# A hybrid decoder step on one core: the first three projection blocks computed together, a quarter of the contraction at a time

## The chip, the cores and the metric

The kernel runs on one core of one Trainium2 chip. The metric is the time of one execution on the device in microseconds (us); of several runs the median is taken. A profile is a separate, recorded execution; its span goes from the first to the last instruction of the core.

The engines by the names that the profile uses: PE is the matrix engine, PEld its weight loads, DVE the vector engine, ACT the scalar engine, POOL the general engine, SP the engine whose queue issues the transfers (SPq).

## The reference, cut to what matters

One layer of a decoder for 304 tokens (16 meta, 256 prompt, 32 sample tokens) of width 2048. The part that the change touches is the very beginning: a norm over the features, and the first columns of the input projection.

```
def rmsnorm(x, g):
    y = x * lax.rsqrt(jnp.mean(x * x, axis=-1, keepdims=True) + EPS)
    return y * g
...
proj = rmsnorm(x, g_mix) @ w_in          # 2048 -> 9248 columns
gate_lru, x_lru, z, xbc_raw, dt_raw = ...   # 2048, 2048, 2048, 3072, 32 columns
xbc = silu(causal_conv(xbc_raw, ...))    # x, B, C of the SSD part
dt = jax.nn.softplus(dt_raw + dt_bias)   # 32 heads
```

After it come the SSD scan, a gated linear recurrence (RG-LRU), an output projection, a squared-ReLU MLP with 8192 hidden features and a final norm. Everything is float32 to float32 accuracy.

## The kernel before, in words

Features lie on the 128 partitions, tokens in the columns. A projection is cut into **blocks** of 128 output features. A block is a sum over 16 feature tiles `k` of 128; since the matrix engine is fed with rounded values (type fp32r), weights and activations are each split into a high part and a low rest, and each `k` takes three matmuls of 128x304: high x high, high x low, low x high. A block is thus 48 matmuls into one bank of the accumulator memory (`gemm`, the matmul is L101).

`prep` brings the weights of a block: a transfer into one of two buffers `wraw` (L78), then ACT makes `whi` (helper `act`, L69) and DVE makes `wlo = wraw - whi` (helper `tt`, L58). `whi` and `wlo` have four buffers of 8 tiles `k`, two for each block. `run_blocks` asks for the weights two blocks ahead. A transfer into `wraw` must wait until ACT and DVE have read the block that lay there.

At the start the input `x` comes in 16 transfers (tiles `big`, L205), one per `k`. The first blocks take x as it comes: ACT makes `x0h` = x times the norm's gain, rounded; DVE makes `x0l`, the rest, in one instruction (helper `stt`, L61). The 1/rms of each token, `rsb`, is multiplied onto the results later. For it the squares of x are summed into `sqx`: eight squares and three additions on POOL, then eight squares on ACT that DVE adds. Matmuls with a column of ones (L161) and a broadcast (L172) turn the sum into `rsb`; only then can the results that are held back be worked on (the posts: `post_dt`, `post_conv`), and the normalized operands `xh`, `xl` of all later blocks be made, in what time DVE has left.

The first block is dt, 32 columns wide. Before, these are copied four times side by side, so that dt is a block like any other, 48 matmuls. Then come the blocks B (`win[0]` to `win[3]`), C and the first four of x. The step size chain on dt (`tables`: softplus, scan, transposes) follows when the held results are released.

The order on each engine is set by a scheduler that orders instructions by a timeline of its own; what it made of both programs is shown with the change. The names with numbers in those rows are single tiles; the profile leaves the numbers out.

Of the kernel before, what the change touches and what calls it, by code (L numbers as in the profile page):

```python
# [28 lines left out]
# columns of the constants  # L29
# [4 lines left out]
def body(ctx, tc, I, O):  # L34
# [38 lines left out]
    # ---------------------------------------------------------------- weights  # L73
# [33 lines left out]
    # blocks: (weights, operands, first column, last column, what follows)  # L107
# [35 lines left out]
    # ---------------------------------------------------------------- constants  # L143
# [14 lines left out]
    # ---------------------------------------------------------------- RMS norm  # L158
# [26 lines left out]
    sqa = sqx[:, 0, :]  # L185
    held, scaled = [], []
# [8 lines left out]
    parts = []  # L195
    for k in range(NK):
        if k % 8 == 0:
            parts.append([wp.tile([P, 8, P], F32R, tag=t, bufs=4, name=nm(t)) for t in ("whi", "wlo")])
        if k % 4 == 0:
            r = rdt[:, k:k + 4, None, :].to_broadcast([P, 4, 4, 32])  # L200
            wh, wl = [t[:, k % 8:k % 8 + 4, :].rearrange("p k (c j) -> p k c j", j=32) for t in parts[-1]]
            act(wh, r, AF.Copy)
            tt(V if k < 8 else G, wl, r, wh.bitcast(F32), SUB)
        xt = bigt()
        SY.dma_start(xt[:], I["x"][:, k, :])  # L205
        xts.append(xt)
        gm = par[:, C_GMIX + k:C_GMIX + k + 1]
        hi = x0p.tile([P, T], F32R, tag="xh", name=nm("x0h"))
        lo = x0p.tile([P, T], F32R, tag="xl", name=nm("x0l"))
        act(hi[:], xt[:], AF.Copy, scale=gm)  # L210
        stt(lo[:], xt[:], gm, hi[:].bitcast(F32), MUL, SUB)
        x0.append((hi, lo))
        if k < 8:
            tt(G, sqx[:, k, :], xt[:], xt[:], MUL)
    for n in (4, 2, 1):
        tt(G, sqx[:, 0:n, :], sqx[:, 0:n, :], sqx[:, n:2 * n, :], ADD)
    ready[id(wdt)] = parts

    def norm_x():
        for k in range(8, NK):  # L220
            sq = sp.tile([P, EXT], F32, tag="th", bufs=2, name=nm("sq"))
            act(sq[:, :T], xts[k][:], AF.Square)
            tt(V, sqa, sqa, sq[:, :T], ADD)
        for _ in range(7):
            yield
# [26 lines left out]
    # ---------------------------------------------------------------- other resident data  # L252
# [9 lines left out]
    hw = cst.tile([P, 152], F32, name="hw")      # halves of conv_ssd_w, conv_ssd_b; lru_ba, lru_bx  # L262
# [42 lines left out]
    # ---------------------------------------------------------------- SSD: B, C, x  # L305
    bf = [sp.tile([P, T], F32, tag="bf", bufs=4, name=f"bf{g}") for g in range(4)]
    cf = [sp.tile([P, T], F32, tag="cf", bufs=4, name=f"cf{g}") for g in range(4)]
# [759 lines left out]
```

## Time and profile before

| | |
|---|---|
| time of 3 runs, median | 1652.5 us (1652.13 to 1656.11) |
| span of the profiled execution | 1649.8 us |
| PE busy | 1625.4 us, 99% of the span |
| DVE, ACT, POOL busy | 64%, 50%, 15% |
| mean granted clock of PE | 0.995 of full speed |
| moved from and to memory | 260.0 and 12.4 MB, 165 GB/s over the span |

The profiled execution's own time is 2.7 us shorter in its span than the median of the runs; what lies around the span is not shown. PE is busy nearly always, so a change can gain or lose only where PE waits or runs at a lower clock: that is at the start (the page cuts the span into 40 slices; PE's digit is 7 in the first and 9 in nearly all others), in one wait of 3.0 us at 126 us, and in the last slice.

### The profile page before, as it was taken

The page shows a single profiled execution, that of the slowest core. Times are in us where ns is not written, and L with a number is a line of the kernel's source. Part 1 is how long each engine was busy: PE and PEld are TensorE (multiplying, and loading weights), DVE is VectorE, ACT ScalarE, POOL GpSimd, SP SyncE. Part 2 cuts the span into 40 slices and gives each one's busy share as a digit, 9 for nine tenths or more (in the row PEclk, how much of TensorE's full clock was granted, in tenths as well). Part 3 has the DMA queues.
Part 4 walks back from the last instruction along what each step waited for, and adds up shares of the span by engine and source line. Part 5 has one row for each costly group of instructions (what it writes and reads, how often), then busy time and mean ns, then how long its engine had stood idle before and what let it go on. Part 6 is the DMA issues. An engine that isn't in the chain of part 4 may idle for free.

```text
span 1649.8 us, 29019 instructions
## 1 busy us (share of the span) xinstructions
PE 1625.4 (99%) x11915; PEld 1587.4 (96%) x11915; DVE 1048.4 (64%) x1542; ACT 830.7 (50%) x1299; POOL 248.0 (15%) x311
## 2 busy tenths in 40 slices
PE   7999999999999999999999999999999999999997
PEld 6998888889999999999999999999999999999997
DVE  7989898988778787556565433544445555545554
ACT  5546575566777775344444433443334433344442
POOL 3433443431223221001140000000000000000000
PEclk9999999999999999999999999999999999999998
DMA  6444555554444455544545444454545454544442
GB/s 215 156 167 139 187 180 180 175 186 142 164 161 164 163 169 180 190 168 160 172 154 170 162 162 170 160 172 157 176 156 176 155 169 163 169 164 161 171 157 105
DMA packets 53989, 274.29 MB, mean 166 GB/s; under 512 B 5984, under 2 KB 12768, under 8 KB 24544
## 3 DMA queue, kind: packets, MB, share of 16 engines
q1 hardware_dynamic: 53856, 272.44, 48.9%
q8 instruction: 93, 1.52, 0.4%
q14 instruction: 40, 0.33, 0.1%
HBM read 259.99 MB, written 12.42 MB: 165 GB/s over the span
## 4 chain that ended last, share of the span: by engine, by line
PE 98%; DMA 1%; DVE 0%; SPq 0%; ACT 0%; issue 0%; DVEq 0%; ACTq 0%
PE g L101 90%; PE s L101 1%; PE s L439 1%; PE s L764 1%; PE s L562 1%; PE s L560 1%; PE s L501 1%; PE s L437 0%; PE s L510 0%; DMA wraw<-in_win 0%; PE s L161 0%; PE s L449 0%; DVE z L58 0%; PE s L172 0%; PE s L521 0%; PE s L587 0%
## 5 line engine op out<-in xcount | busy, mean ns | idle before, releaser
L58 DVE TENSOR_TENSOR wlo<-wraw,whi 128x1024 fp32r<-128x1024 f32 (+1 forms) x470 | 573.3, 1221 | 443.8 <-ACT whi L69 443.2
L69 ACT ACTIVATE whi<-wraw 128x1024 fp32r<-128x1024 f32 (+1 forms) x470 | 492.4, 1049 | 683.6 <-PE g L101 630.3
L101 PE MATMUL g<-mh,whi 128*128 128x288 f32 x1024 | 303.2, 296 | 0.0
L101 PE MATMUL g<-hh,whi 128*128 128x288 f32 x1024 | 303.0, 296 | 0.0
L101 PE MATMUL g<-hl,whi 128*128 128x288 f32 x1024 | 302.4, 295 | 0.0
L101 PE MATMUL g<-ml,whi 128*128 128x288 f32 x1024 | 302.1, 295 | 0.0
L101 PE MATMUL g<-hh,wlo 128*128 128x288 f32 x1024 | 301.3, 294 | 0.0
L101 PE MATMUL g<-mh,wlo 128*128 128x288 f32 x1024 | 301.1, 294 | 0.0
L101 PE MATMUL g<-xh,whi 128*128 128x288 f32 (+1 forms) x960 | 288.3, 301 | 3.0 <-DVE ext L288 3.0
L101 PE MATMUL g<-xl,whi 128*128 128x288 f32 (+1 forms) x960 | 287.4, 300 | 0.0
L101 PE MATMUL g<-xh,wlo 128*128 128x288 f32 (+1 forms) x960 | 286.8, 299 | 0.0
L101 PEld LDWEIGHTS g<-mh,wlo 128*128 128x128 f32 x1024 | 192.9, 188 | 0.0
L101 PEld LDWEIGHTS g<-hh,wlo 128*128 128x128 f32 x1024 | 192.8, 188 | 0.0
L101 PEld LDWEIGHTS g<-hh,whi 128*128 128x128 f32 x1024 | 192.5, 188 | 0.0
L101 PEld LDWEIGHTS g<-hl,whi 128*128 128x128 f32 x1024 | 192.5, 188 | 0.0
L101 PEld LDWEIGHTS g<-ml,whi 128*128 128x128 f32 x1024 | 192.3, 188 | 0.0
L101 PEld LDWEIGHTS g<-mh,whi 128*128 128x128 f32 x1024 | 191.9, 187 | 0.0
L101 PEld LDWEIGHTS g<-xh,whi 128*128 128x128 f32 x960 | 180.3, 188 | 6.9 <-DVE ext L288 3.2
L101 PEld LDWEIGHTS g<-xl,whi 128*128 128x128 f32 x960 | 180.4, 188 | 3.9 <-issue 1.0
L101 PEld LDWEIGHTS g<-xh,wlo 128*128 128x128 f32 x960 | 180.6, 188 | 2.8 <-issue 0.2
L101 PE MATMUL g<-lh,whi 128*128 128x288 f32 x256 | 75.8, 296 | 0.0
L101 PE MATMUL g<-sh,whi 128*128 128x288 f32 x256 | 75.7, 296 | 0.0
(272 smaller groups left out, 2327.7 us busy)
## 6 DMA issues: line engine op xcount, KB each, us to landing
wraw<-in_win SPq DMA_DIRECT2D x69, 1024.0 KB, 5.0
wraw<-in_wup SPq DMA_DIRECT2D x64, 1024.0 KB, 4.9
wraw<-in_wdn SPq DMA_DIRECT2D x64, 1024.0 KB, 4.9
wraw<-in_wout SPq DMA_DIRECT2D x32, 1024.0 KB, 4.9
h<-in_stssd SPq DMA_DIRECT2D x32, 256.0 KB, 3.0
out_sssd<-h SPq DMA_DIRECT2D x32, 256.0 KB, 3.5
wraw<-in_win SPq DMA_DIRECT2D x12, 256.0 KB, 5.2
big<-in_x SPq DMA_DIRECT2D x16, 152.0 KB, 3.6
```

The source lines that it names most:

```text
L58: e.tensor_tensor(out, a, b, op=op)
L69: A.activation(out, in_, f, **kw)
L101: TE.matmul(o, a[:, k % 8, :], b[:, c0:c1], start=n == 0, stop=n == 3 * NK - 1)
L439: TE.matmul(po[0:66, :], cm[:, 66 * b:66 * b + 66], a[:], start=b == 0 and n == 0, stop=b == 7 and n == 1)
L501: TE.matmul(pbc[:, 0:NT], selr[:, h:h + 1].to_broadcast([64, P]), acst[:], start=True, stop=True)
L560: TE.matmul(py[64 * q:64 * q + 64, 128 * c:128 * c + 128], xdc[c][:, 64 * j:64 * j + 64], em[c][:, j, :], start=True, stop=True)
L562: TE.matmul(py[:, 256 + 128 * c:384 + 128 * c], hst[c][:, 128 * t:128 * t + 128], C[:, 16 + 128 * c:144 + 128 * c], start=True, stop=True)
L764: TE.matmul(pr[:, :FL], w_[:, m, :], x_[:], start=n == 0, stop=n == 2)
```

## The change

It alters the start only; later parts are the same code (comments were dropped, so line numbers move).

- dt's high and low parts lie side by side: one operand `wd` of 64 columns for each `k` (66 are taken, the last two belong to the next tile). Each `k` takes two matmuls, with `x0h` and `x0l`, instead of three; dt is 32 matmuls. Its result has two halves of 32 rows, which `tables` adds and copies four times in one float32 matmul with a selection matrix (`s4`, `px`).
- dt, `win[0]` and `win[1]` run together (`run_first`): a quarter of the contraction (4 `k`) of dt, then of `win[0]`, then of `win[1]`, then the next quarter. Loads follow that order: 4 tiles of x, a quarter of the weights of both blocks, and so on; so do the splits on ACT and DVE.
- `x0l` is made in two DVE instructions: `xg` = x times gain (one operand tile, one buffer), then `xg - x0h`.
- The squares of the last eight tiles are made by ACT into the still unused tiles `bf`, `cf`, early, and all eight are added by POOL, not DVE. POOL's two instructions for dt's `wlo` go.
- Nine float32 matmuls of 128x128 on ones run at the very start (`wps`), before any data is there.
- `norm_x` takes fewer steps before the sum of squares is used, `tables` one more.

```diff
+    wps = bank()
+    for _ in range(9):
+        TE.matmul(wps[:, 0:P], ones[:].to_broadcast([P, P]), ones[:].to_broadcast([P, P]), start=True, stop=True)
...
+    first = [[], []]
+    wd = x0p.tile([P, 64 * NK + 2], F32R, tag="wd", bufs=1, name="wd")
+    wd3 = wd[:, 0:64 * NK].rearrange("p (k j) -> p k j", j=64)
...
     for k in range(NK):
-        if k % 8 == 0:
-            parts.append([wp.tile([P, 8, P], F32R, tag=t, bufs=4, name=nm(t)) for t in ("whi", "wlo")])
-        if k % 4 == 0:
-            r = rdt[:, k:k + 4, None, :].to_broadcast([P, 4, 4, 32])
-            wh, wl = [t[:, k % 8:k % 8 + 4, :].rearrange("p k (c j) -> p k c j", j=32) for t in parts[-1]]
-            act(wh, r, AF.Copy)
-            tt(V if k < 8 else G, wl, r, wh.bitcast(F32), SUB)
...
+        if m == 0:
+            wh, wl = wd3[:, k:k + 8, 0:32], wd3[:, k:k + 8, 32:64]
+            act(wh, rdt[:, k:k + 8, :], AF.Copy)
+            tt(V, wl, rdt[:, k:k + 8, :], wh.bitcast(F32), SUB)
...
         act(hi[:], xt[:], AF.Copy, scale=gm)
-        stt(lo[:], xt[:], gm, hi[:].bitcast(F32), MUL, SUB)
+        V.tensor_scalar(xg[:], xt[:], gm, None, op0=MUL)
+        tt(V, lo[:], xg[:], hi[:].bitcast(F32), SUB)
         x0.append((hi, lo))
         if k < 8:
             tt(G, sqx[:, k, :], xt[:], xt[:], MUL)
+        else:
+            act((bf + cf)[k - 8][:], xt[:], AF.Square)
+        if k % 4 == 3:
+            q = slice(k - 3, k + 1)
+            for f, raw, ap in zip(first, raws, win):
+                SY.dma_start(raw[:, q, :], ap[:, q, :])
+                wh, wl = [t[:, m - 3:m + 1, :] for t in f[-1]]
+                act(wh, raw[:, q, :], AF.Copy)
+                tt(V, wl, raw[:, q, :], wh.bitcast(F32), SUB)
     for n in (4, 2, 1):
         tt(G, sqx[:, 0:n, :], sqx[:, 0:n, :], sqx[:, n:2 * n, :], ADD)
-    ready[id(wdt)] = parts
+    for t in bf + cf:
+        tt(G, sqa, sqa, t[:], ADD)
+
+    def run_first(posts):
+        pss_ = [bank() for _ in range(3)]
+        for q in range(4):
+            ks = range(4 * q, 4 * q + 4)
+            for k in ks:
+                for n, b in enumerate(x0[k]):
+                    TE.matmul(pss_[0][0:66, :T], wd[:, 64 * k:64 * k + 66], b[:],
+                              start=k == 0 and n == 0, stop=k == NK - 1 and n == 1)
+            for f, ps in zip(first, pss_[1:]):
+                for k in ks:
...
     def norm_x():
-        for k in range(8, NK):
-            sq = sp.tile([P, EXT], F32, tag="th", bufs=2, name=nm("sq"))
-            act(sq[:, :T], xts[k][:], AF.Square)
-            tt(V, sqa, sqa, sq[:, :T], ADD)
-        for _ in range(7):
+        for _ in range(3):
             yield
...
-    def tables(x0):
+    def tables(y0):
+
+        yield
+        px = bank()
+        s4 = sp.tile([64, 4, 32], F32, tag="dup", bufs=1, name="s4")
+        V.tensor_copy(s4[:], con[0:64, None, K_SEL:K_SEL + 32].to_broadcast([64, 4, 32]))
+        TE.matmul(px[:, :T], flat(s4), y0[0:64, :],
+                  start=True, stop=True)
```

On DVE, at the start, the program before has one instruction for each `x0l`, all 16 in a row, and the weights' splits after them (`x0l_99` is that of k=0, `x0l_161` that of k=8):

```order
L61 SCALAR_TENSOR_TENSOR x0l_99<-big_96,par,x0h_98 128x304
L61 SCALAR_TENSOR_TENSOR x0l_106<-big_103,par,x0h_105 128x304
L61 SCALAR_TENSOR_TENSOR x0l_113<-big_110,par,x0h_112 128x304
L61 SCALAR_TENSOR_TENSOR x0l_120<-big_117,par,x0h_119 128x304
L61 SCALAR_TENSOR_TENSOR x0l_129<-big_126,par,x0h_128 128x304
```

In the changed program the same place reads as follows, from the first tile to k=3 (`wlo_115` and `wlo_117` are the low parts of `win[0]` and `win[1]`):

```order
L226 TENSOR_SCALAR xg_124<-big_120,par 128x304
L58 TENSOR_TENSOR x0l_123<-xg_124,x0h_122 128x304
L226 TENSOR_SCALAR xg_133<-big_129,par 128x304
L58 TENSOR_TENSOR x0l_132<-xg_133,x0h_131 128x304
L226 TENSOR_SCALAR xg_142<-big_138,par 128x304
L58 TENSOR_TENSOR wlo_115<-wraw_112,whi_114 128x512
L58 TENSOR_TENSOR x0l_141<-xg_142,x0h_140 128x304
L58 TENSOR_TENSOR wlo_117<-wraw_113,whi_116 128x512
L226 TENSOR_SCALAR xg_151<-big_147,par 128x304
L58 TENSOR_TENSOR x0l_150<-xg_151,x0h_149 128x304
```

Each `x0l` is now two rows, and the quarters of `wlo` stand between them. From the row of `xg_124` to that of `x0l` for k=8 there are 24 rows, to the last `wlo` of `win[0]` 31, to the last `x0l` 41.

On PE, in the changed program, this is the place where k=8 begins (`s_318` is dt's bank, `s_319` and `s_320` those of `win[0]` and `win[1]`; `x0h_212`, `x0l_213` belong to k=8):

```order
L251 MATMUL s_318<-x0h_212,wd 66x304
L258 MATMUL s_319<-x0h_212,whi_204 128x304
L258 MATMUL s_320<-x0h_212,whi_206 128x304
L251 MATMUL s_318<-x0l_213,wd 66x304
L251 MATMUL s_318<-x0h_221,wd 66x304
L258 MATMUL s_319<-x0l_213,whi_204 128x304
L258 MATMUL s_319<-x0h_212,wlo_205 128x304
```

Before, dt's 48 matmuls stood ahead of those of `win[0]`; now all three blocks take each tile as it comes. From the row of `x0l_213` on, 61 of the 128 matmuls of the three blocks are left; ahead of the last five stands the sum of squares (L161 of before), and behind them the block `win[2]`.

On POOL, before, these rows stand between the first two squares and the first addition:

```order
L58 TENSOR_TENSOR wlo_155<-rdt,whi_154 128x512
L58 TENSOR_TENSOR sqx<-big_110 128x304
L58 TENSOR_TENSOR sqx<-big_117 128x304
L58 TENSOR_TENSOR wlo_155<-rdt,whi_154 128x512
L58 TENSOR_TENSOR sqx<-big_126 128x304
```

In the changed program POOL's rows after the eight squares are:

```order
L58 TENSOR_TENSOR sqx<-sqx 128x1216
L58 TENSOR_TENSOR sqx<-sqx 128x608
L58 TENSOR_TENSOR sqx<-sqx 128x304
L58 TENSOR_TENSOR sqx<-sqx,bf_87 128x304
L58 TENSOR_TENSOR sqx<-sqx,bf_88 128x304
L58 TENSOR_TENSOR sqx<-sqx,bf_89 128x304
L335 COPY ext_307<-stsc 128x8x3
L335 COPY ext_309<-stsc 128x8x3
L335 COPY ext_311<-stsc 128x8x3
L58 TENSOR_TENSOR sqx<-sqx,bf_90 128x304
```

Four more additions follow. POOL's two rows for `wlo` are gone and eight additions are new, so that it has 22 instructions up to the end of the sum: 8 squares, 3 additions in the tree, 8 more, 3 copies.

## Rows read from the trace of the kernel before

**Rows 1.** The page's busy times, share of the span and instructions of each engine.
```profile
PE 1625.4 (99%) x11915; PEld 1587.4 (96%) x11915; DVE 1048.4 (64%) x1542; ACT 830.7 (50%) x1299; POOL 248.0 (15%) x311
```
**Rows 2.** What PE waited for: us in total, times, longest us.
```profile
PE s L101 <- ACT x0h L69: 6.3, 1, 6.3
PE s L101 <- DVE x0l L61: 3.9, 5, 2.3
PE g L101 <- DVE ext L288: 3.0, 1, 3.0
```
**Rows 3.** Stretches: us, busy us (instructions) by engine, granted clock, DMA share, GB/s.
```profile
6.30:15.10 8.80, 7.81 (x24) 6.08 (x25) 8.78 (x9) 8.07 (x19) 8.78 (x9) 1.00 0.99 315
15.10:20.90 5.80, 2.82 (x12) 1.99 (x10) 5.80 (x4) 2.90 (x5) 5.41 (x3) 0.80 0.84 303
...
25.10:46.40 21.30, 21.30 (x155) 21.30 (x155) 12.33 (x24) 10.53 (x20) 0.51 (x2) 0.99 0.49 154
```
**Rows 4.** The chain that ended last, in order of time: start us, us, what.
```profile
31.98 6.42 PE g L101 x46
38.41 0.56 PE s L161 x6
...
42.42 0.60 PE s L172 x6
...
46.43 78.31 PE g L101 x569
```
**Rows 5.** POOL and DVE in order of time: start us, us, instruction, merged count.
```profile
5.50 1.34 POOL L58 TENSOR_TENSOR sqx<-big 128x304 f32<-128x304 f32 x2 [5.06 <-DMA big<-in_x]
...
11.51 3.57 POOL L58 TENSOR_TENSOR sqx<-big 128x304 f32<-128x304 f32 x4
...
15.15 5.57 POOL L58 TENSOR_TENSOR sqx<-sqx 128x1216 f32<-128x1216 f32 x3
...
14.45 6.61 DVE L61 SCALAR_TENSOR_TENSOR x0l<-big,par,x0h 128x304 fp32r<-128x304 f32 x4
...
21.18 1.29 POOL L292 COPY ext<-stsc 128x24 f32<-128x24 f32 x3 [0.45 <-DMA stsc<-in_stsc]
```
**Rows 6.** Single tiles up to 46 us: duration ns min/median/max, first and last start.
```profile
L61 DVE SCALAR_TENSOR_TENSOR x0l<-big,par,x0h x16: 517/960/3035, 6.3 to 22.3; 128x304 fp32r<-128x304 f32 x16
...
L58 DVE TENSOR_TENSOR wlo<-wraw,whi x14: 672/675/1225, 22.8 to 43.4; 128x512 fp32r<-128x512 f32 x12, 128x1024 fp32r<-128x1024 f32 x2
...
L69 ACT ACTIVATE whi<-wraw x14: 615/631/1059, 13.5 to 42.3; 128x512 fp32r<-128x512 f32 x12, 128x1024 fp32r<-128x1024 f32 x2
...
L58 POOL TENSOR_TENSOR sqx<-sqx x3: 946/1589/2877, 15.2 to 19.8; 128x1216 f32<-128x1216 f32 x1, 128x608 f32<-128x608 f32 x1, 128x304 f32<-128x304 f32 x1
```
**Rows 7.** PE in order of time, two stretches: start us, us, instruction.
```profile
23.05 0.46 PE L101 MATMUL s<-x0h,wlo 128*128 128x304 f32 x1
23.30 0.46 PE L101 MATMUL s<-x0h,whi 128*128 128x304 f32 x1
...
28.05 0.30 PE L101 MATMUL s<-x0h,whi 128*128 128x304 f32 x1
28.19 0.30 PE L101 MATMUL s<-x0l,whi 128*128 128x304 f32 x1
```
**Rows 8.** DVE in order of time, later: start us, us, instruction.
```profile
121.29 0.48 DVE L58 TENSOR_TENSOR big<-th 128x304 f32<-128x304 f32 x1
121.69 0.31 DVE L278 TENSOR_SCALAR th<-big 128x304 f32<-128x304 f32 x1
121.91 0.31 DVE L274 TENSOR_SCALAR big<-big 128x304 f32<-128x304 f32 x1
122.26 0.48 DVE L61 SCALAR_TENSOR_TENSOR big<-big,big 128x304 f32<-128x304 f32 x1
```
**Rows 9.** The page's DMA issues: count, KB each, median us to landing.
```profile
wraw<-in_win SPq DMA_DIRECT2D x69, 1024.0 KB, 5.0
```
**Rows 10.** A later stretch, columns as in Rows 3.
```profile
44.55:120.80 76.25, 76.25 (x556) 76.25 (x555) 70.60 (x146) 42.57 (x65) 32.88 (x46) 1.00 0.49 164
```

More of the change, by code (lines that the diff above doesn't have):

```diff
@@ L185, in body @@
     sqa = sqx[:, 0, :]
+    bf = [sp.tile([P, T], F32, tag="bf", bufs=4, name=f"bf{g}") for g in range(4)]
+    cf = [sp.tile([P, T], F32, tag="cf", bufs=4, name=f"cf{g}") for g in range(4)]
     held, scaled = [], []
@@ L194, in body @@
     SY.dma_start(par[:], I["par"])
-    parts = []
-    for k in range(NK):
-        if k % 8 == 0:
-            parts.append([wp.tile([P, 8, P], F32R, tag=t, bufs=4, name=nm(t)) for t in ("whi", "wlo")])
-        if k % 4 == 0:
-            r = rdt[:, k:k + 4, None, :].to_broadcast([P, 4, 4, 32])
-            wh, wl = [t[:, k % 8:k % 8 + 4, :].rearrange("p k (c j) -> p k c j", j=32) for t in parts[-1]]
-            act(wh, r, AF.Copy)
-            tt(V if k < 8 else G, wl, r, wh.bitcast(F32), SUB)
+    first = [[], []]
+    wd = x0p.tile([P, 64 * NK + 2], F32R, tag="wd", bufs=1, name="wd")
+    wd3 = wd[:, 0:64 * NK].rearrange("p (k j) -> p k j", j=64)
+    V.memset(wd[:, 64 * NK:].bitcast(F32), 0.0)
+    raws = [wp.tile([P, NK, P], F32, tag="wraw", bufs=2, name=nm("wraw")) for _ in range(2)]
+    for k in range(NK):
+        m = k % 8
+        if m == 0:
+            for f in first:
+                f.append([wp.tile([P, 8, P], F32R, tag=t, bufs=4, name=nm(t)) for t in ("whi", "wlo")])
+        if m == 0:
+            wh, wl = wd3[:, k:k + 8, 0:32], wd3[:, k:k + 8, 32:64]
+            act(wh, rdt[:, k:k + 8, :], AF.Copy)
+            tt(V, wl, rdt[:, k:k + 8, :], wh.bitcast(F32), SUB)
         xt = bigt()
@@ L214, in body @@
             tt(G, sqx[:, k, :], xt[:], xt[:], MUL)
+        else:
[7 more added lines that the diff above has]
+                tt(V, wl, raw[:, q, :], wh.bitcast(F32), SUB)
     for n in (4, 2, 1):
         tt(G, sqx[:, 0:n, :], sqx[:, 0:n, :], sqx[:, n:2 * n, :], ADD)
-    ready[id(wdt)] = parts
-    def norm_x():
-        for k in range(8, NK):
-            sq = sp.tile([P, EXT], F32, tag="th", bufs=2, name=nm("sq"))
-            act(sq[:, :T], xts[k][:], AF.Square)
-            tt(V, sqa, sqa, sq[:, :T], ADD)
-        for _ in range(7):
+    for t in bf + cf:
[10 more added lines that the diff above has]
+                for k in ks:
+                    hi, lo = f[k // 8]
+                    xh, xl = x0[k]
+                    for n, (a, b) in enumerate(((hi, xh), (hi, xl), (lo, xh))):
+                        TE.matmul(ps[:, :T], a[:, k % 8, :], b[:], start=k == 0 and n == 0,
+                                  stop=k == NK - 1 and n == 2)
+        blocks[0] += 3
+        done.extend(range(3))
+        for ps, post in zip(pss_, posts):
+            held.append(lambda post=post, ps=ps: post(ps))
+        pump()
+    def norm_x():
+        for _ in range(3):
             yield
@@ L610, in post_x @@
         return f
-    for w in win[0:2]:
-        ready[id(w)] = prep(w, 4)
-        done.append(id(w))
     SY.dma_start(con[:], I["con"])
     SY.dma_start(stsc[:], I["stsc"])
-    ph1 = [(wdt, x0, 0, T, post_dt)]
+    ph1 = []
     for g in range(4):
@@ L623, in body @@
         ph1.append((win[8 + o], x0, 0, T, post_x(o)))
-    run_blocks(ph1, win[12:14])
+    run_first([post_dt] + [b[4] for b in ph1[:2]])
+    run_blocks(ph1[2:], win[12:14])
     while len(xa) < NK:
```

8 lines of the change are left out of this document (4 added, 4 removed).

## The prediction

> **What bounds the kernel now.** I read the page first: PE is busy 1625.4 of 1649.8 us [rows 1]. Only 24.4 us are PE's idle time, so the next view is what PE waited for: 6.3 us for the first tile, 3.9 us in five waits for `x0l` from DVE, 3.0 us once at 126 us for an accumulator bank [rows 2]; the rest, some 11 us, lies at the very end, which the change leaves alone. The stretches then show that the start loses more than these waits. From 25.1 to 46.4 us PE is busy without a gap at full clock, but in the six microseconds from 15.1 it did 2.8 us of work at a mean clock of 0.80 [rows 3]. A matmul of 128x304 follows the one before by 0.25 us at 23 us and by 0.14 us at 28 us [rows 7]: these are PE's two levels, 1.2 and 2.4 GHz.
>
> Why was PE idle there? DVE was busy all the time, with `x0l`. One such instruction takes 0.52 us at its shortest, 0.96 us in the middle and 3.04 us at worst [rows 6]. The long ones lie beside POOL's: four squares on POOL took 3.57 us, 0.89 each, where two took 1.34 us before DVE began; the three additions of the tree took 5.57 us, and DVE finished only three or four `x0l` in them [rows 5]. In the stretch from 6.3 to 15.1 us both engines are busy throughout, and each has nine instructions [rows 3]. So a DVE instruction that reads two tiles and a POOL instruction take turns, one for one, and DVE goes at POOL's pace. That is the pattern on which my sum rests.
>
> **The point of comparison.** Before, at 46.43 us four blocks, the sum of squares and the broadcast are done [rows 4]. A block takes 6.70 us (46 matmuls in 6.42 us, 0.1396 each), the broadcast 0.60 us. Without the fourth block and the broadcast, "three blocks and the sum of squares done" is 39.1 us. In the changed program I look for S, the time at which `win[2]` can run without a stop; all that follows is the same PE work, except for one float32 matmul.
>
> **The change, part by part.**
>
> *POOL.* Squares 8 x 0.89 = 7.1 us from 5.5 us, tree 5.6 us, eight new additions of the width of the tree's last, which takes 0.95 us, so 1.0 us with its start: 8.0 us; three copies 1.3 us [rows 5, 6]. The two `wlo` go. POOL ends at about 27.5 us, after 22 instructions.
>
> *DVE.* Each `x0l` becomes a multiplication and a subtraction. Without POOL the multiplication is 0.31 us, and an instruction that needs its result follows 0.35 us after its start; one behind a subtraction follows after 0.40 us [rows 8]. So a pair costs some 0.71 us, a quarter's `wlo` 0.6 to 0.67 us [rows 6]. The subtraction reads two tiles, as `x0l` did, and takes turns with POOL. Whether the multiplication, which reads one tile, waits too is seen in no row. Bounds: at its own 0.31 us if it never waits, at a full turn of POOL, 0.9 to 1.0 us, if it does. The nearest rows are those of `x0l` itself: same input tile, same per-partition factor, same partner; I take the waiting.
> The Trainium skill's page "SBUF — State Buffer", section "Who interferes with whom", says that DVE instructions with two SBUF inputs contend with POOL's reads, and that `tensor_scalar` can contend as well when it runs in a two-port mode. By that rule the multiplication waits and the sum is the one below; if only the first half of it applied, it would be the first rival's. No row here shows the second half.
>
> So DVE does 22 instructions while POOL does 22, up to 27.5 us. The `x0l` of k=8 is the 24th row: 28.2 us. Seven rows on (three multiplications, two subtractions, a copy of 0.2, the last `wlo` of `win[0]`), 2.5 us at DVE's own pace, `wraw` is read: 30.7 us. The last `x0l` comes 17 rows after that of k=8, at 34.6 us.
>
> *PE.* At the place of k=8 the order stands still until 28.2 us; 61 matmuls and the sum of squares (0.56 us) are left: 61 x 0.1396 + 0.56 = 9.1 us, so 37.3 us. That dt has 32 matmuls and not 48 is in this count (16 x 0.14 = 2.2 us).
>
> *Weights of `win[2]`.* The transfer waits for the buffer, 30.7 us, lands 5.0 us later [rows 9]; ACT's `whi` of 1024 columns takes 1.06 us, DVE's `wlo` 1.22 us [rows 6]: 38.0 us. The third matmul needs it, two may go ahead. S = 37.7 us, the later of the two: 1.4 us earlier than 39.1.
>
> *The added matmul `px`.* 304 float32 columns. The broadcast has 304 columns in three pieces, 0.60 us [rows 4]; at most that: -0.6 us. Below: nothing, if it fell into a wait.
>
> *At nothing:* the nine warm-up matmuls lie in the 6.3 us in which PE has no data [rows 2]; without that cover nine at the broadcast's 0.2 us (128 columns) would be 1.8 us, 3.6 us at the lower clock. ACT's squares are the same eight, earlier; ACT had 0.7 us idle of 8.8 there [rows 3] and waits less for banks of `whi` later. SP issues the same transfers in another order; total bytes are the same, so the last quarter of weights comes when it came before, long before DVE gets to it. DVE's eight additions (3.8 us at 0.48, [rows 8]) are off its list, but the eight more rows of multiplications put more on it.
>
> *Later.* `rsb` needs `win[2]` and a quarter of `win[3]`; DVE splits two more blocks first, so the held results start at about S + 10 = 48 us against 44.6. From there to the last `xl` DVE was 70.6 us busy in 76.3 us [rows 10]; in the changed order one `wlo` of 1.2 us and the start of the step size chain fall outside. At some 74 us it ends near 122 us. PE needs it after ten blocks, the broadcast and 139 of the next three blocks' 144 matmuls: S + 67.0 + 0.6 + 19.4 = 124.7 us, so no wait. The 3.0 us wait for a bank [rows 2] stands at the same seam, where ACT's and DVE's splits are ahead of the copy out of the bank; I leave it, with 2 us either way for the range.
>
> Sum: -1.4 + 0.6 = -0.8 us. Against the profiled span: 1649.0 us; the median of the runs is 2.7 us above the span, so 1651.7 us.
>
> **The rivals.**
>
> 1. *The multiplication does not wait.* Then k=8's `x0l` is the 15th instruction that takes turns; POOL's 15th ends at 5.5 + 7.1 + 5.6 + 4.0 + 1.3 = 23.5 us. Three turns more (two subtractions, the last `wlo` of `win[0]`): 26.7. Weights 26.7 + 5.0 + 1.06 + 1.22 - 0.3 = 33.7, PE 23.5 + 9.1 = 32.6 us. S = 33.7, 5.4 us earlier, less `px`: 1647.7 us. For it: it reads one tile only. Against: its 0.31 us for 304 columns against the subtraction's 0.48 [rows 8] say it reads faster than one column at a time, perhaps by the second way in.
> 2. *DVE and POOL hardly meet*, since the new order spreads x over more time. Then DVE's 41 rows take 16 x 0.71 + 8 x 0.61 + 0.2 = 16.4 us, and the transfers set the pace: `stsc` landed at 21.2 us [rows 5], and 0.67 MB of `con` and `stsc` at 303 GB/s [rows 3] are 2.2 us, so the last quarter of weights is there by 19.0; 19.0 + 1.2 (its split) + 5.0 + 2.0 is S = 27.2, 11.9 us earlier: 1641.2 us. Against: POOL has more to do than before, from the first tile on.
> 3. *Slower: the clock.* PE waits for 4 us or so beside the tree, then for each `x0l`; before, after a wait of 2.3 us there, it ran at 1.2 GHz. If the 61 matmuls from 28.2 us run at 0.25 us each, that is 15.3 + 0.6 us, S = 44.1: 1652.5 + 5.0 + 0.6 = 1658.1 us. Each matmul at the lower clock costs 0.11 us, and there is 1.2 us to lose (0.4 to the weights, 0.8 of gain), so it decides from 11 of them on; about half of the 61 would give 1655. For it: the mean clock of 0.80 there [rows 3]. Against: after 28.2 us nothing interrupts PE, and before, the clock was back for good by 25.1 us [rows 3], within five microseconds of the last wait.
> The Trainium skill's page "TensorE: Matmul & The Clock Gate", part 1, calls the throttled state the default, released by sustained activity. By it the warm-up at the start is lost in the wait that follows, and this rival's loss is bounded.
> 4. *The change does not do what it says*: the wait for `x0l` goes, and a wait for the weights of `win[2]` takes its place. That is in my forecast, 0.4 us; each further microsecond of that transfer, which shares the queues with that of `win[3]`, is one of the time, and 3 us give 1654.7.
>
> **How the numbers follow.** Forecast 0.52 (1649.5 to 1654); rival 1 0.20; rival 2 0.08; rival 3 0.13; rival 4 0.07. A measurement here tells about 0.3% from no change, 5 us: below 1647.5 faster, above 1657.5 slower. Faster: rival 2, half of rival 1, a little of the forecast, should the wait at 126 us go: 0.21. Slower: a third of rival 3: 0.05. The rest, 0.74, is within. The range from 1646.0 to 1655.5 leaves out rival 2, the lower end of rival 1 and the worse half of rival 3.
>
> **What would show it.** In the changed profile: DVE's multiplications at 0.9 us and more beside POOL (mine) or at 0.31 (rival 1); POOL's sum ending near 27.5 us; PE standing at k=8's `x0l` until 28; `win[2]`'s first matmul near 37.5 us and a full stretch behind it at clock 1.00 (a lower one is rival 3); the bank wait still near 125 us. The prediction is wrong if DVE gets more than one instruction into each of POOL's, or if a wait comes up after 50 us that I have not seen.

## The result, and the profile after: slower by 0.8%

The changed kernel took 1665.5 us (median of 4 runs, 1665.1 to 1667.3); beside it the kernel before took 1652.3 us. The ratio is 1.0078, 95% interval 1.0064 to 1.0092: 13 us slower, where the forecast was 1651.7 and the range ended at 1655.5. One run of the kernel before, beside the experiments e10 to e13, took 2642.0 us at a mean granted clock of 0.557 and is left out throughout.

The first row answers to [rows 1]; the last is the granted clock by slices of 41.6 us, in tenths.

```profile
PE 1634.2 (98%) x11919; PEld 1593.4 (96%) x11919; DVE 1049.3 (63%) x1550; ACT 829.4 (50%) x1295; POOL 246.5 (15%) x317
...
PEclk8998998999999999999999999999999999999998
```

PE is idle for 28.8 us of a span of 1663.0 us, before for 24.4; that is 4.4 us of the 13.2. PE was also busy 8.8 us longer: it has 16 large matmuls less to do, but nine warm-up matmuls (4.2 us) and `px` more, and the row of the clock says where it ran slower: slices 4 and 7, at 125 to 166 and 250 to 291 us, are below their neighbours. (In this one record full clock reads 0.949; matmuls follow each other by 0.139 us there as before, and the other three runs show 0.99 in the mean.) What PE waited for, as in [rows 2]:

```profile
PE s L251 <- DVE x0l L58: 7.3, 5, 3.7
PE g L101 <- DVE ext L331: 3.8, 2, 2.0
PE s L488 <- ACT h0h L69: 2.0, 1, 2.0
...
PE s L412 <- DVE t1d L370: 0.9, 1, 0.9
...
PE s L486 <- DVE h L58: 0.7, 1, 0.7
PE s L412 <- DVE big L405: 0.6, 1, 0.6
PE g L101 <- DVE wlo L58: 0.4, 1, 0.4
```

The `x0l` waits are the start. L331 is the copy out of a bank, once at the seam (126.3 us; as in the prediction, the place three blocks behind the first matmul with `xh`) as before, and once more at 158.6. L412 are the transposes of the step size chain (`tables`), L486 and L488 matmuls of the SSD stage at 263 and 268 us. The rows of L412, L486 and L488 have no counterpart before. The stretches between, columns as in [rows 3]:

```profile
105.25:129.44 24.19, 22.37 (x157) 21.52 (x156) 17.26 (x36) 12.99 (x22) 11.15 (x18) 0.95 0.42 135
129.44:132.85 3.41, 3.41 (x16) 3.41 (x15) 2.75 (x5) 0.60 (x2) 1.90 (x4) 0.50 0.90 358
160.16:163.57 3.41, 3.04 (x12) 3.07 (x13) 3.38 (x11) 2.63 (x7) 1.72 (x7) 0.50 0.91 303
265.97:276.21 10.24, 9.55 (x39) 7.08 (x40) 8.96 (x19) 2.42 (x5) 4.86 (x5) 0.50 0.70 237
```

Three stretches, 17.1 us in all, ran at half clock, each at the end of one of the waits or just behind it. A microsecond at half clock loses half a microsecond of work, so they cost 8.5 us. The kernel before has none between 25.5 and 1640 us.

So an account can be kept for each kernel: the time at which the first matmul with `xh` starts (the second phase; 105.80 us before), plus PE's waits from there to 390 us, plus half the half-clock time there, plus 0.9 us for `px` where it stands in that stretch (the block with it took 7.55 us instead of 6.65). Before, the span less the first two is 1649.8 - 105.8 - 3.0 = 1541.0 us, all the rest. For the changed kernel: 1541.0 + 105.25 + 7.9 + 8.5 + 0.9 = 1663.6, against a span of 1663.0. **The start gained 0.55 us, where 1.4 was forecast; everything that was lost was lost later.**

The place is the step size chain. DVE in order of time at the seam (columns as in [rows 5]):

```profile
114.93 1.23 DVE L58 TENSOR_TENSOR wlo<-wraw,whi 128x1024 fp32r<-128x1024 f32 x1 [0.71 <-ACT whi L69]
116.07 0.47 DVE L58 TENSOR_TENSOR xl<-big,xh 128x304 fp32r<-128x304 f32 x1
116.46 0.53 DVE L284 SCALAR_TENSOR_TENSOR big<-big,par,rsb 128x304 f32<-128x304 f32 x1
117.51 0.48 DVE L58 TENSOR_TENSOR xl<-big,xh 128x304 fp32r<-128x304 f32 x1 [0.52 <-ACT xh L69]
...
126.77 1.22 DVE L58 TENSOR_TENSOR wlo<-wraw,whi 128x1024 fp32r<-128x1024 f32 x1 [3.65 <-ACT whi L69]
...
135.87 0.53 DVE L386 TENSOR_SCALAR big<-s,par 128x304 f32<-128x304 f32 x1
...
139.18 2.05 DVE L314 RECIPROCAL th<-th 128x304 f32<-128x304 f32 x1
...
158.07 0.16 DVE L370 COPY t1d<-big 64x32 f32<-64x32 f32 x1
```

DVE stands idle in front of the seam, 6.9 us of the 24.2 from 105 us on, while the chain is not begun: its reciprocal starts at 139.2 us (118.4 before) and `t1d` is written at 158.2 (140.6 before). On PE the transposes that read it moved too: from the start of the second phase to the first matmul with `t1d` there are 240 block matmuls before and 336 now, five blocks and seven. Two blocks behind the seam, before:

```profile
118.42 2.04 DVE L271 RECIPROCAL th<-th 128x304 f32<-128x304 f32 x1
...
140.42 0.16 DVE L329 COPY t1d<-big 64x32 f32<-64x32 f32 x1
...
142.92 0.28 PE L363 MATMUL s<-con,t1d 64*128 64x64 f32 x1
```

And four blocks behind it now, where PE stands three times:

```profile
156.22 0.30 PE L101 MATMUL g<-xh,wlo 128*128 128x304 f32 x1
157.09 0.34 PE L412 MATMUL s<-con,big 64*128 64x64 f32 x2 [0.56 <-DVE big L405]
158.29 0.27 PE L412 MATMUL s<-con,t1d 64*128 64x64 f32 x1 [0.87 <-DVE t1d L370]
160.53 0.59 PE L101 MATMUL g<-xh,whi 128*128 128x304 f32 x1 [1.98 <-DVE ext L331]
```

The last row's 0.59 us is the lower clock already. Without the first two waits PE would be at `t1d` at 156.9 us, 13.9 us later than before; the chain is 17.6 us later. At 263 us a load of the SSD state is late; the chain that ended last shows it as a store, the load behind it, and PE:

```profile
256.14 5.23 DMA out_sssd<-h
...
261.39 2.96 DMA h<-in_stssd
...
264.43 0.64 ACT h0h L69
...
265.11 0.44 PE s L488
```

### The profile page after: what moved, and what is told of

It reads as the page before. It is cut to its first block, busy times and chain, and to the rows that moved or that the text cites. A ratio compares the mean times of both kernels' runs of the same rounds, so it can differ in the third digit from the quotient of the medians.

```text
span 1663.0 us, 29029 instructions
## 1 busy us (share of the span) xinstructions
PE 1634.2 (98%) x11919; PEld 1593.4 (96%) x11919; DVE 1049.3 (63%) x1550; ACT 829.4 (50%) x1295; POOL 246.5 (15%) x317
## 4 chain that ended last, share of the span: by engine, by line
PE 95%; DVE 2%; DMA 1%; issue 1%; ACT 0%; SPq 0%; DVEq 0%; ACTq 0%
PE g L101 89%; PE s L488 1%; PE s L811 1%; PE s L611 1%; PE s L609 1%; DMA wraw<-in_win 1%; PE s L550 1%; DVE wlo L58 0%; PE s L486 0%; PE s L559 0%; PE s L498 0%; DVE x0l L58 0%; DMA out_sssd<-h 0%; DVE z L58 0%; PE s L172 0%
```

## The experiments

**Theory A** at the outset: the one step (a `yield`) that the change adds at the head of `tables` sends the chain behind the seam, and all of the loss follows from it. **Rival B**: the new order of the start makes the loss, whatever dt's layout and steps. **Rival C**: the late state load is a loss by itself. All runs at a glance; the four columns behind the ratio are the account of the profiled execution, whose sum stands beside its span.

| kernel | median us | ratio to before, 95% | phase 2 from | waits | half clock | sum | span |
|---|---|---|---|---|---|---|---|
| before | 1652.3 | | 105.8 | 3.0 | 0 | | 1649.8 |
| changed | 1665.5 | 1.0078 (1.0064 to 1.0092) | 105.3 | 7.9 | 17.1 | 1663.6 | 1663.0 |
| e4 changed, no added step | 1655.6 | 1.0016 (1.0006 to 1.0025) | 105.4 | 3.3 | 6.8 | 1654.0 | 1654.8 |
| e1 changed, dt four copies | 1662.6 | 1.0053 (1.0036 to 1.0071) | 108.6 | 4.3 | 10.2 | 1659.1 | 1661.0 |
| e5 changed, `x0l` in one | 1663.0 | 1.0061 (1.0038 to 1.0085) | 104.3 | 8.9 | 23.9 | 1667.0 | 1666.2 |
| e9 no added step, `x0l` in one | 1654.8 | 1.0006 (0.9997 to 1.0016) | 106.4 | 3.3 | 3.4 | 1653.3 | 1653.6 |
| e10 no added step, norm sooner | 1655.0 | 1.0013 (1.0003 to 1.0022) | 105.7 | 3.1 | 3.4 | 1652.4 | 1653.5 |
| e12 e9, norm sooner | 1654.9 | 1.0013 (1.0003 to 1.0023) | 105.3 | 3.1 | 6.8 | 1653.7 | 1654.7 |
| e7 before, added step | 1658.6 | 1.0025 (1.0015 to 1.0035) | 104.8 | 4.8 | 6.8 | 1654.0 | 1652.9 |
| e3 before, dt side by side, added step | 1657.1 | 1.0024 (1.0013 to 1.0034) | 101.5 | 7.0 | 17.1 | 1658.9 | 1657.3 |
| e6 e3 without the step | 1647.3 | 0.9958 (0.9943 to 0.9974) | 101.8 | 0 | 3.4 | 1645.4 | 1645.2 |
| e8 e6, `px` at once | 1650.7 | 0.9981 (0.9969 to 0.9994) | 103.4 | 2.5 | 3.4 | 1648.6 | 1649.2 |
| e13 e6, norm sooner | 1646.7 | 0.9964 (0.9951 to 0.9977) | 101.8 | 0 | 3.4 | 1645.4 | 1644.8 |
| e11 e6, `x0l` in two | 1650.2 | 0.9979 (0.9970 to 0.9988) | 104.7 | 0.3 | 3.4 | 1648.6 | 1648.4 |
| e15 e6, squares added by POOL | 1650.7 | 0.9978 (0.9969 to 0.9988) | 105.1 | 0.3 | 0 | 1647.3 | 1648.2 |
| e14 e6, blocks run together | 1649.1 | 0.9970 (0.9960 to 0.9981) | 99.0 | 3.3 | 6.8 | 1647.6 | 1647.6 |
| e16 e14, series shorter | 1653.7 | 1.0003 (0.9991 to 1.0016) | 99.2 | 6.5 | 10.2 | 1652.7 | 1652.5 |
| e17 e14, series shorter still | 1653.5 | 1.0007 (0.9996 to 1.0017) | 100.0 | 4.5 | 13.7 | 1652.3 | 1651.1 |

The sums meet the spans to about 2 us, so the account holds. (In e8 and e17 `px` runs ahead of the second phase, so it is in its start.) The other runs of before beside them lay between 1651.2 and 1657.4 us, with a median from 1652.2 to 1654.4, so differences between kernels that were not run side by side are read from the ratios too. The account is of one execution, the time a median of several.

**e4, the added step alone taken out.**

```diff
     def tables(y0):
-
-        yield
         px = bank()
```

> The changed kernel without the one added yield at the head of `tables`; everything else of the change stays. Theory A (the whole loss is that the step size chain comes behind the seam at 126 us, so that PE stands at its transposes at 156 us, and waits and half-clock stretches follow up to 276 us): the chain's RECIPROCAL starts before 121 us as before, no wait of PE at the transposes, no half clock between 30 and 390 us, and the time falls by 13.2 us to 1652 us (1650 to 1655). Rival B (the loss comes from the new order of the start, whatever dt's layout and steps): no difference that tells, 1665 us. Rival C (the state load behind the stores at 263 us is a loss by itself: 2.7 us of waits and 5.1 us of half clock): 1665.5 - 13.2 + 7.8 = 1660 us.

Measured 1655.6 us: 9.9 us of the 13.2 are the step's (10.2 by the ratios). Its waits and its stretch ahead of the seam:

```profile
PE s L251 <- DVE x0l L58: 6.8, 5, 3.1
PE g L101 <- DVE ext L331: 3.3, 1, 3.3
```

```profile
105.40:130.62 25.22, 21.95 (x154) 21.11 (x153) 23.42 (x47) 13.59 (x24) 9.34 (x16) 1.00 0.45 139
130.62:134.03 3.41, 3.41 (x16) 3.41 (x15) 3.41 (x6) 0.65 (x2) 3.41 (x5) 0.50 0.71 228
```

DVE is now busy 23.4 of 25.2 us ahead of the seam, with the chain: its reciprocal starts at 117.4 us. `px` ran on PE at 109.7 us, against 109.5 in the changed kernel, so it isn't `px` that the chain waited for; the step alone moved DVE's instructions, and PE's transposes with them (222 block matmuls into the phase here). In every kernel with the step there are 336 of them ahead of the transposes with `t1d`, in every one without 200 to 273. The waits at the transposes and for the state load are gone, the latter with nothing done about it: rival C falls, and B for most of the loss. What is left is a wait at the seam like that of before, now with half clock behind it. Why the scheduler puts the chain on DVE so much later for one step is not in any trace.

**e1, dt as before in the changed kernel** (four copies in tiles of `ah`, `al`, which are still unused; 48 matmuls).

```diff
-                for n, b in enumerate(x0[k]):
-                    TE.matmul(pss_[0][0:66, :T], wd[:, 64 * k:64 * k + 66], b[:],
-                              start=k == 0 and n == 0, stop=k == NK - 1 and n == 1)
+                xh, xl = x0[k]
+                for n, (j, b) in enumerate(((0, xh), (0, xl), (1, xh))):
+                    TE.matmul(pss_[0][:, :T], wd[k // 2][j][:, P * (k % 2):P * (k % 2) + P], b[:],
...
-        yield
-        px = bank()
```

> The changed kernel with dt as before: four copies side by side, 48 matmuls, no `px` and no added step; the three blocks still run together. Theory A: 1665.5 - 13.2 us, less 0.6 us for `px`, more 1.1 us for the eight matmuls of dt that lie behind the last long wait for `x0l` (the other eight fall into waits): 1653 us (1650 to 1656), no half clock between 30 and 390 us. Rival B: 1665 us or more, with the wait at the transposes still there. Rival C: 1660 us.

1662.6 us: a miss for A as it was written. The chain is early (reciprocal at 119.7 us) and PE has no wait at the transposes, but phase 2 begins 3.4 us later, and at the seam 4.3 us of waits and 6.8 us of half clock come up. So the step isn't all: the rest of the change has a cost of its own.

**e3 and e6, dt's layout alone**, in the kernel before, with the added step and without it. Of the edit only dt's matmuls are shown; `wd`, `s4` and `px` are those of the change.

```diff
+            if w is None:
+                for b in (xh, xl):
+                    TE.matmul(ps[0:66, :T], wd[:, 64 * k:64 * k + 66], b[:], start=n == 0, stop=n == 2 * NK - 1)
+                    n += 1
...
     def tables(y0):
+        yield
```

> The kernel before with dt's two parts side by side alone (`wd`, 32 matmuls, `px`, the added step); the three blocks run one after the other, `x0l` is one instruction, DVE adds the squares. Theory A: the chain starts behind the seam again, so some 13 us of waits and half clock come up between 126 and 390 us; start about as before or up to 2 us shorter: 1652.5 + 12 = 1664 us (1660 to 1667). Rival B: 1652 us, no half clock between 30 and 390 us.

> The kernel before with dt's two parts side by side and `px`, without the added step. The third block began 4.3 us earlier at 105 us with dt's layout alone. If the added step is what delays the chain here too, the waits at 149, 224 and 262 us and their half clock go, the wait for a bank at the seam comes back with up to 3.4 us of half clock behind it as in the changed kernel without the step: 1652.3 - 4.3 + 0.9 for `px` + 0 to 3 = 1650 us (1648 to 1652.5). If the waits belong to dt's layout and `px` themselves, 1657 us as with the step.

1657.1 and 1647.3 us: the step costs 9.8 us here too (10.9 by the ratios), as in the changed kernel. e3's waits are of the same family:

```profile
PE g L108 <- DVE ext L293: 2.0, 1, 2.0
PE s L573 <- DVE yo L58: 1.8, 1, 1.8
PE s L474 <- POOL bd L334: 1.4, 1, 1.4
...
PE s L376 <- DVE t1d L334: 0.9, 1, 0.9
```

Of e6 all waits are these four, the last two at the end of the kernel:

```profile
PE s L101 <- ACT x0h L69: 5.1, 1, 5.1
PE s L101 <- DVE x0l L61: 3.6, 4, 2.2
PE s L168 <- ACT sr L69: 1.0, 1, 1.0
PE s L179 <- DVE rf L983: 0.8, 1, 0.8
```

Phase 2 begins 4 us sooner, the last `xl` is written at 114.8 us (120.8 before, 123.1 changed), and the wait at the seam is gone. The layout with its step left out beats both kernels.

**e7, the step alone**, in the kernel before: one `yield` at the head of `tables`, nothing else.

```diff
     def tables(x0):
+        yield
```

> The kernel before with one yield more at the head of `tables` and nothing else: the step size chain is written one quarter block later, each engine's work is the same. If the step alone sends the chain behind the seam, PE stands at the transposes and what follows, and the time rises by some 10 us to 1662 us (1658 to 1665), with the RECIPROCAL of the chain after 130 us (118.4 before). If the chain is late because it has to wait for `px`, nothing is lost: 1652 us.

1658.6 us, 0.25% slower, less than expected. The reciprocal starts at 132.7 us, so the step alone does send the chain behind the seam. PE waits 4.8 us for `tok`, `em`, `yo` and the state's parts between 152 and 261 us, but the 3.0 us at the seam are gone. The profiled execution is the fastest of the ten (1654.7 us) and its span only 3.1 us longer than that of before, so the account leaves some of the median open. What the step costs depends on the kernel around it: 0.25% here, 0.62 and 0.66% in the other two.

**e5 and e9, `x0l` in one instruction**, in the changed kernel with the step and without.

```diff
-        V.tensor_scalar(xg[:], xt[:], gm, None, op0=MUL)
-        tt(V, lo[:], xg[:], hi[:].bitcast(F32), SUB)
+        stt(lo[:], xt[:], gm, hi[:].bitcast(F32), MUL, SUB)
```

> The changed kernel with `x0l` made by one DVE instruction again. If each DVE instruction costs a turn of POOL, the one of k=8 is the 15th or 16th to take turns and not the 24th; POOL's 15th ended at 23.6 us in the changed kernel, so PE goes on at about 24 us and not at 29, and the three blocks end some 4 us earlier. Nothing is changed in the step size chain, whose waits at 156 and 263 us should stay: 1661 us (1659 to 1664). If POOL's instructions alone set the pace, or the weights' transfers, nothing is won at the start: 1665 us.

> The changed kernel with `x0l` in one instruction and without the added step. `x0l` in one instruction began the second phase 1.0 us earlier (104.27 against 105.25 us), though its three blocks ended 4.9 us earlier, since the weights of `win[2]` came 3.3 us late. If that 1.0 us adds to what the step gave: 1655.6 - 1.0 = 1654.6 us (1653 to 1656). If the tail's waits move with the start: outside of that.

1663.0 us (e5's profiled run was its slowest, 1668.2) and 1654.8 us. e9 is at the time expected, but not by the way expected: its second phase begins 1.0 us later than e4's, and one half-clock stretch less makes up for it. The start of e5, PE in order of time:

```profile
32.14 0.73 PE L161 MATMUL s<-ones,sqx 128*128 128x1 f32 x6
35.43 0.41 PE L101 MATMUL g<-x0h,whi 128*128 128x304 f32 x1 [2.56 <-ACT whi L69]
...
36.69 0.62 PE L101 MATMUL g<-x0h,wlo 128*128 128x304 f32 x1 [0.71 <-DVE wlo L58]
```

The sum of squares comes at 32.1 us, 4.9 us sooner than in the changed kernel, as forecast from the turns; 3.3 us of it go to the weights of `win[2]`, the prediction's rival 4.

**e8, e10, e12, e13: is it the norm that is late?** e8 writes `px` where the held results are released; e10 and e12 drop the three steps ahead of the sum of squares in `norm_x`, e13 three of seven (e8, e10, e13):

```diff
+        tt(V, y0[0:64, :], ps[0:64, :T], rsb[0:64, :], MUL)
+        px = bank()
...
         gens.append(tables(x0))
```

```diff
-        for _ in range(3):
-            yield
         ms = bank()
```

```diff
-        for _ in range(7):
+        for _ in range(4):
             yield
```

> The kernel before with dt's two parts side by side, and `px` run at once when the held results are released, ahead of the long series of `xh` and `xl`; no added step. The chain on DVE depends on nothing late, so it should start before the seam: no wait at the transposes; 1652.3 - 4.3 + 0.6 + 0 to 3 for the seam = 1650 us (1647 to 1652). If the layout costs the tail by itself: 1657 us.

> The changed kernel without the added step, and `norm_x` without its three steps ahead of the sum of squares, so that the broadcast of 1/rms is written three quarter blocks (5 us) sooner; `rsb` was there at 48.3 us, and at 38.5 us with dt's layout alone. Theory D (what the rest of the change costs is DVE's lateness: the held results, the 16 `xl` and the chain all wait for `rsb`; the last `xl` ended at 125.1 us against 114.8, and the seam's wait and clock follow from that): last `xl` near 120.5 us, the time falls by about 4 us to 1651.5 us (1649 to 1654). Rival E (running together costs by PE's waits at the start alone, or the seam is chance): 1655.6 us.

> The changed kernel without the added step, `x0l` in one instruction, and `norm_x` without its three first steps (1654.8 us with them). Theory D: the sum of squares stood at 32.1 us with `x0l` in one instruction, so that here the broadcast can come 5 us or more sooner than 49: last `xl` near 120 us, 1650 us (1648 to 1653). Rival E: 1654.8 us.

> The fastest kernel so far (dt's parts side by side, no added step, 1647.3 us) with four steps instead of seven ahead of the sum of squares in `norm_x`. Theory D: `rsb` at 38.5 us can come up to 3 us sooner, but nothing waits at the seam any more, so little is to be had: the half clock at 145.7 us (1.7 us) at most: 1645.5 to 1647.5 us. If the order at the seam is chance, up to 1651 us with a wait for a bank.

e8 kept the gain of e6 only in part (a wait of 2.2 us at the seam; its runs spread from 1647.5 to 1654.6 us). In e10 `rsb` came 4.0 us and the last `xl` 2.3 us sooner than in e4, and the time fell by 0.6 us, which is nothing that can be told: the wait at the seam stayed at 3.1 us. e12 gave nothing either. Theory D, that the lateness of `rsb` sets what is left, falls as it was put: sooner by two or four microseconds is not enough. e13 did as expected, 1646.7 us, the best time of all, not to be told from e6.

**e11, e14, e15: the other parts, one at a time on e6.** e11 has `x0l` in two instructions; e15 the squares of the last eight tiles made early by ACT and added by POOL; e14 the three blocks run together (`run_first` and its order of loads) with `x0l` in one instruction and the additions on DVE, no warm-up matmuls (`norm_x` has the three steps of the change).

```diff
-        stt(lo[:], xt[:], gm, hi[:].bitcast(F32), MUL, SUB)
+        V.tensor_scalar(xg[:], xt[:], gm, None, op0=MUL)
+        tt(V, lo[:], xg[:], hi[:].bitcast(F32), SUB)
```

```diff
+        else:
+            act((bf + cf)[k - 8][:], xt[:], AF.Square)
...
+    for t in bf + cf:
+        tt(G, sqa, sqa, t[:], ADD)
```

```diff
-    run_blocks(ph1, win[12:14])
+    run_first([post_dt] + [b[4] for b in ph1[:2]])
+    run_blocks(ph1[2:], win[12:14])
```

> The kernel before with dt's two parts side by side, no added step (1647.3 us), and `x0l` made by two DVE instructions as in the changed kernel; additions of the squares on DVE, blocks one after the other, no warm-up. Theory D: DVE has 16 instructions more at the start, the 16 `x0l` end some 5 us later than 19.9, `rsb` and the last `xl` come 4 to 6 us later and the time rises to 1651.5 us (1650 to 1654). Rival E: the three or four microseconds of PE's waits at the start are taken by the same waits, 1648 us.

> dt's parts side by side without the added step (1647.3 us), and of the rest of the change only the running together of the three blocks with its order of loads: `x0l` is one instruction, DVE adds the squares, no warm-up. Theory F (running together by itself costs: both weight buffers stay taken up to the last quarter, so that the weights of `win[2]` come 3 us late, and the broadcast of 1/rms stands behind `win[2]`, so that `rsb`, the last `xl` and the seam come late): `rsb` near 47 us, a wait of 3 us for a bank at the seam, 1654 us (1652 to 1656). Rival G (the additions on POOL are what costs, through their turns with DVE): 1648.5 us.

> dt's parts side by side without the added step (1647.3 us), and of the rest of the change only the squares made early by ACT and added by POOL; blocks one after the other, `x0l` in one instruction. Theory F: POOL is done with the additions by 28 us at the latest, about when the third block ends (28.2 us), so the sum waits little: 1648.5 us (1646.5 to 1651). Rival G: the turns delay `x0l` and the sum, 1652 us or more.

Each alone is slower than e6: 2.9, 1.8 and 3.4 us, in the order e11, e14, e15 (the runs of e14, 1646.8 to 1651.3 us, overlap those of e6). But the places differ. e11 and e15 begin phase 2 some 3.0 and 3.3 us later: PE waits 7.9 us for `x0l` in e11 against 3.6 in e6, and in e15 seven times against four, with the half clock of the start lasting to 27.1 us against 22.8. That is DVE and POOL taking turns. e14 begins phase 2 at 99.0 us, sooner than any kernel before it: running together is a gain of 2.7 us, and my theory F, which had it as the cost at the start with `rsb` near 47 us, is wrong there (`rsb` came at 42.4); the wait at the seam that it named did come. e9 differs from e14 by the additions on POOL, ACT's early squares and the warm-up, and begins at 106.4 us. The first row is `x0l` of e14, the second that of e9 (ns min/median/max):

```profile
L61 DVE SCALAR_TENSOR_TENSOR x0l<-big,par,x0h x16: 520/529/3057, 6.1 to 24.5; 128x304 fp32r<-128x304 f32 x16
```

```profile
L61 DVE SCALAR_TENSOR_TENSOR x0l<-big,par,x0h x16: 520/964/3075, 6.3 to 29.3; 128x304 fp32r<-128x304 f32 x16
```

With POOL's additions beside it the median `x0l` takes 964 ns instead of 529. Not all of the 7.4 us between the two starts is these turns: ahead of phase 2 the record has 10.2 us at half clock in e9 and 3.4 in e14, which is 3.4 us of it, and e5, with the same start as e9 but the step, begins 5.2 us behind e14. What e14 won is lost at the seam: a wait of 3.3 us and 6.8 us at half clock.

**e16 and e17: can e14 keep its 6.8 us?** The series of `xh` and `xl` is written in fewer steps (two for eleven of the tiles, or for all, instead of three):

```diff
             xa.append((hi, lo))
             yield
             yield
-            yield
+            if k > 10:
+                yield
```

> Running together alone, with dt's layout and without the added step, took 1649.1 us; its second phase began at 99.0 us (105.8 before), and a wait of 3.3 us for a bank and two half-clock stretches at the seam took half of that back. Here the series of `xh` and `xl` has two steps for each of the first eleven tiles and three for the rest, so that it is written out when the last block of the phase ends, not in one lump at the seam. If the lump makes the wait: no wait at the seam, 99.0 us kept, 1645 us (1643 to 1647). If the wait comes of the start being early, whatever the series: 1649 us.

> The same with two steps for each of the 16 tiles, so that the series is written out a block and a quarter ahead of the seam. If the lump makes the wait: none at the seam, 1645 us (1643 to 1647). If the wait comes of the start being early: 1649 us.

1653.7 and 1653.5 us: neither theory gives this time. The last `xl` is there at 113.8 and 108.6 us; the wait at the seam shrinks to 2.4 us in e16 and is gone in e17 (its 0.9 us for a bank come at 134 us, behind the transposes), as the first theory had it. But the stall comes up in the SSD stage instead, at 247 to 268 us, near where the changed kernel has its own. The chain that ended last in e16:

```profile
248.84 5.13 DMA out_sssd<-h
...
254.38 3.19 DMA out_sssd<-h
257.58 2.92 DMA h<-in_stssd
```

PE is held there by stores and loads of the state: each load waits until the store out of one of four tiles (`h0`) is through. It is not simply that PE comes early: block matmul 700 of the second phase starts at 235.5 us in e16, 237.4 in e17 and 236.4 in e6, which does not wait there. A fifth tile wasn't tried, and why e6 escapes stays open.

## Why the prediction was wrong

**Turns of DVE and POOL, and the multiplication: right.** `xg` waits for POOL although it reads one tile. The first row is DVE's, the second POOL's tree, whose first addition it spans; away from POOL an `xg` takes 0.38 us. POOL ended its 22nd instruction at 27.8 us (forecast 27.5), DVE its 22nd at 28.0 and its 24th, the `x0l` of k=8, at 29.0 (forecast 28.2).

```profile
13.40 2.81 DVE L226 TENSOR_SCALAR xg<-big,par 128x304 f32<-128x304 f32 x1
```

```profile
13.11 5.69 POOL L58 TENSOR_TENSOR sqx<-sqx 128x1216 f32<-128x1216 f32 x3
```

So rivals 1 and 2 fall. The sentence of the Trainium skill's page "SBUF — State Buffer", section "Who interferes with whom", by which `tensor_scalar` can contend too, agrees with this trace. (Rival 1 was also added up wrongly: its 23.5 us are the end of POOL's 18th instruction, not the 15th, since its list has three copies that the count leaves out. With the 15th at 21.6 its time would have been 1645.8 us. The expectation of e5 has the same slip.)

**The start: right in its path, smaller in its gain.** `x0l` of k=8 released PE at 29.0 us (forecast 28.2), the sum of squares came at 37.1 (37.3), the third matmul of `win[2]` at 39.2 (38.0), and phase 2 began 0.55 us sooner (forecast 1.4). Most of the difference is the 0.8 us by which `x0l` of k=8 came late. `px` took 0.9 us, more than the 0.6 that were to be the most. The half clock from 20.2 to 27.0 us was over before k=8: rival 3 did not come. The warm-up matmuls, from 0.9 to 5.1 us, did not bring the clock up for the first data: from 9.1 to 13.2 us the matmuls still followed each other by 0.25 us.

**Later, to the last `xl`: right.** The held results start at 48.6 us (forecast 48), the last `xl` ends at 123.1 (122), and PE does not wait for it.

**The step that failed is the next half sentence of "Later".** "In the changed order one `wlo` of 1.2 us and the start of the step size chain fall outside": I used it to fit DVE's work into the stretch and gave it no price. Taking the chain out of the stretch moved its start from 118.4 to 139.2 us and its end from 140.6 to 158.2, and I did not ask who waits for it. Before, `t1d` ends at 140.6 and PE reads it at 142.9 us: 2.3 us of slack. The matmul that reads it moved back two blocks, 13.9 us, and the chain 17.6, so the slack became a wait of 1.4 us. PE waits there (3.4 us with the copy behind it), and in the SSD stage behind it once more for the state and for DVE (2.7 us), with 13.7 us at half clock behind both. e4 and e6 show that one step sets this: 9.9 and 9.8 us. That the waits of the SSD stage follow from the late transposes is not shown by itself: they go with the step in e4 and e6, but e16 and e17 have such waits without it. This is the second half of the prediction's closing condition, a wait behind 50 us that I had not seen.

**The wait at the seam: within its allowance.** I left its 3.0 us with 2 us either way. It took 1.8 us and 1.7 us for half clock in the changed kernel, 3.3 and 1.7 without the step, and none in e6. In the changed kernel the copy out of the bank, at 127.92 us, stands on DVE behind a `wlo` that waited for ACT up to 126.77; what sets it in the others was not found.

**What the forecast could not tell apart.** That the start moved by half a microsecond hid three larger terms: by the start of phase 2, dt's layout gave 4.0 us (e6), running together 2.7 more (e14), and the additions on POOL (with the early squares and the warm-up, which were not parted) took 7.4 of it back (e9 against e14, with 3.4 us of half clock in it; 5.2 by e5). They don't add up without rest, since the turns and the wait for `win[2]` cover each other: `x0l` in two costs 3.0 us in e11, but with the additions on POOL its removal gave 1.0 us in e5 and lost 1.0 in e9.

**What stays open.** Why the schedule of e6 has no wait at the seam and that of e4 3.3 us. The traces show the last `xl` at 114.8 and 125.1 us, and waits of 0 to 2.4 us where it came before 119.5 (with e14, 3.3 us at 118.7, as an exception) and 1.8 to 4.0 where it came later; the experiments on it (e10, e12, e16, e17) brought the `xl` sooner and the time no lower. A version that keeps e14's start was not found.

## What to carry to other kernels

When a change moves the start of a chain on an engine that is not the bound, look up where the bound engine reads the chain's last result, and compare how far the two move, even if it lies 100 us behind the change: here the chain came 17.6 us later and its reader 13.9, with 2.3 us of slack between them. A step added to a generator is a change of the schedule and deserves a run of its own; without it the part of this change that saved work was 0.4% faster than the kernel before. And a gain at the start of a kernel of many stages is only kept if the next stage that is bound elsewhere can begin sooner too.

## What the runs showed of the hardware

A short wait can cost half as much again, or nothing more. In the profile of before PE waited 3.0 us at the seam and went on at full clock; in e4 it waited 3.3 us and ran 3.4 us at half clock from 0.9 us behind the wait's end. The runs of the one program before differ in the same way, though where each lost its clock is not recorded: those with a mean granted clock of 0.997 took 1651.2 to 1652.8 us, those with 0.992 took 1655.9 to 1657.0.

Half clock also came without a wait. In e6 PE was busy throughout, and the clock fell at 145.7 us, behind the chain's small matmuls of 32 columns, 22 of them from 142.9 to 145.5 us. The kernel before and e15 have the same 22 matmuls, from 146.8 and 144.6 us on, with full clock behind them, so these do not settle it either. The first row is most of the 22 in e6, the others are stretches with the columns of [rows 3]:

```profile
L388 PE MATMUL s<-tok,con x16: 270/272/292, 143.6 to 145.3; 32*128 32x32 f32 x16
```

```profile
138.00:145.70 7.70, 7.70 (x59) 7.41 (x58) 7.64 (x19) 4.91 (x12) 3.96 (x7) 1.00 0.42 137
145.70:149.12 3.42, 3.42 (x19) 3.12 (x17) 2.35 (x6) 1.58 (x5) 1.56 (x3) 0.50 0.01 2
```

The record of the clock starts with its first change, at 15.2 us in the kernel before and at 22.8 in e6. What stands ahead of it reads 1.00: so in the first row of [rows 3], though the matmuls of 128x304 from 9.1 to 11.1 us follow each other by 0.25 us and more, the spacing of the lower clock.
